# Moving the row sums of four modulation vectors from the DeltaNet heads to the branch merge of a hybrid encoder layer

## The chip, the cores and the metric

The kernel runs on one core of a Trainium2 chip. The metric is the device time of one execution in microseconds (us), as a median over runs. TensorE (PE in the profile) multiplies matrices, VectorE (DVE), ScalarE (ACT) and GpSimd (POOL) work elementwise, and SyncE (SP) issues the DMAs. PE reads from the on-chip memory SBUF and writes to eight PSUM banks of 128 x 512 floats.

## The reference, cut to what matters

One layer with 1024 tokens and a width of 1024. A conditioning vector `c` gives six modulation vectors of 1024 each:

```
mod = silu(c) @ w_ada + b_ada
shift_t, scale_t, gate_t, shift_f, scale_f, gate_f = split(mod, 6)
h = x * (1 + scale_t) + shift_t
proj = h @ w_in            # DeltaNet q,k,v,z; attention q,k,v; merge gates ...
merged = gate_a * (o_a @ w_branch_a) + gate_b * (o_b @ w_branch_b)
x = layernorm(ALPHA * x + gate_t * (merged @ w_o))
h = x * (1 + scale_f) + shift_f
x = layernorm(ALPHA * x + gate_f * ffn(h))
```

`o_a` comes from eight heads of a gated delta rule, `o_b` from sixteen heads of band attention. The first two vectors are needed at once. The last four, `gate_t`, `shift_f`, `scale_f` and `gate_f`, are 4096 columns of `w_ada` (16.8 MB) that are not needed before the output projection `w_o`. The change is about these four.

## The kernel before, in words

The kernel passes through these stages: the first two modulation vectors and `h`; the eight DeltaNet heads; attention in eight pairs of heads; the merge, sixteen branch blocks (eight of `w_branch_a`, then eight of `w_branch_b`); the output projection `mix` with the first layer norm; the up-projection; the down-projection.

Matrices are multiplied as three products of a high and a low part. A weight block of 128 x 1024 floats is loaded into a place called `raw`, ACT casts it to the high part `wh` (L177), and POOL or DVE subtracts to get the low part `wl` or the like (L180). The pool `W` has nine places of 512 KB, W0 to W8: three for `raw` (W0 to W2), three for `wh` (W3 to W5), three for `wl` (W6 to W8). Each call of `W.tile(..., tag="raw", bufs=RB)` takes the next of its three in turn. `place("W0", ...)` names a place directly, and `ring(key, ...)` takes the next place of the list that the table `AT` has under the key. `pbank(name, ring)` does the same with PSUM banks, by the table `RINGS`; there `"po"`, `"i"` and `"mod"` are all bank 7.

The order of the instructions on each engine is made by a planner ahead of the run: it goes through the program with priorities (earlier lines first, some stages raised) and a model of costs, and it puts in every wait. SP issues all DMAs of these stages in one list.

In the heads, `mod_rows(i)` (L803 to L826) is called twice for each head, i from 0 to 15. The 4096 columns are eight strips of 512, and each strip takes two halves of four row blocks of 128. A half loads two raws of 512 KB (L811) from the three-place ring and makes four VectorE passes over 128 x 512 (L816 for the first, L818 for the others), each adding `silu(c)` times a row block to an accumulator in the ring `gt`, which has two places and is shared with the evictions of the merge gates. After an odd half, a matmul with a matrix of ones sums over the 128 partitions (L822, tile `pmod`, bank 7), the bias row is loaded (L824), added (L825) and the strip is stored to `mod_d` in DRAM (L826). Bank 7 is in the heads that of `stage_inverse` too.

In the merge (from L1036), block j of branch br takes its weights by `wblock` (L1041), and two groups of 24 matmuls (L1047) make 512 columns each. The gates come from DRAM (L1051); DVE multiplies (L1053, L1055) and in branch B POOL adds both branches (L1056). At blocks 5, 6 and 7 the eight operands `ob_d` of branch B are loaded and split (L1064); in branch B the eight blocks of `w_o` are loaded (L1073), scaled by `gate_t` (L1074, from `mod_d`) and split. PE works on branch A while attention is still running, since the planner fills with it what attention leaves.

After `mix(0)` and `mix(1)`, `shift_f` and `scale_f` are loaded from `mod_d` as sixteen rows of 128 (L1116), transposed on PE (L1118) and combined with the layer norm's vectors in `aff`.

Of the kernel before, what the change touches and what calls it, by code (L numbers as in the profile page):

```python
# [73 lines left out]
def _at(group, step_, n, first=0):  # L74
# [27 lines left out]
    "bt": _at("GA", 640, 2), "sb": (*_at("GA", 640, 4, 1280), ("FA", 384)),  # L102
    "ot": (("GA", 3840), ("FA", 0)), "mx": _at("FA", 4, 8, 256),

    "gb": _at("GB", 512, 2), "macc": _at("M", 0, 1), 
    "st": _at("ST", 12, 2), "mv": _at("ST", 4, 4, 36), "gtb": (MA[0],), "g1b": (_E1[1],),
    "b1b": (_E1[2],), "r": (_E1[3], ("GL", 0)), "x1": _at("GL", 1024, 2, 1024),
    "h2": _at("GL", 0, 1, 3072),
# [45 lines left out]
def hybrid_layer(  # L154
# [646 lines left out]
    macc = [None]  # L801

    def mod_rows(i):  # L803

        cb = i // 2
        if i % 2 == 0:
            macc[0] = ring("gt", [P, 512])
        acc = macc[0]
        for k0 in range(4 * (i % 2), 4 * (i % 2) + 4, 2):
            rv = W.tile([P, 2, 512], F32, tag="raw", bufs=RB, name=nm("raw"))  # L810
            SP.dma_start(rv, w_ada2[k0 * P:(k0 + 2) * P,  # L811
                                    2 * D + 512 * cb:2 * D + 512 * cb + 512].rearrange(
                                        "(k p) n -> p k n", p=P))
            for k in (k0, k0 + 1):
                if k == 0:
                    DVE.tensor_scalar(acc, rv[:, 0, :], csil[:, 0:1], None, ALU.mult)  # L816
                else:
                    DVE.scalar_tensor_tensor(acc, rv[:, k - k0, :], csil[:, k:k + 1], acc,  # L818
                                             ALU.mult, ALU.add)
        if i % 2 == 1:  # L820
            pr_ = mtile(nm("pmod"), "i")
            PE.matmul(pr_, ones, acc, start=True, stop=True)  # L822
            row = ring("gt", [P, 512])[0:1, :]
            SP.dma_start(row, b_ada[:, 2 * D + 512 * cb:2 * D + 512 * cb + 512])  # L824
            DVE.tensor_tensor(row, row, pr_[0:1, :], ALU.add)  # L825
            SP.dma_start(mod_d[:, 512 * cb:512 * cb + 512], row)  # L826
# [13 lines left out]
    for h in range(HA):  # L840
        ORD = "sigKq"
        for o in ORD:
            if o == "s":
                with tc.high_priority(offset=PF):
                    stage_solve(h, cs[h])
            elif o == "i":
                with tc.high_priority(offset=PI):
                    stage_inverse(h, cs[h])
            elif o == "K" and h + 1 < HA:
                with tc.issue_after(last.ins) if last else nullcontext():  # L850
                    cs.append(stage_k(h + 1))
            elif o == "g":
                some_gates(GA[h])
            elif o == "q" and h + 1 < HA:
                stage_q(h + 1, cs[h + 1])
        some_gates(GB[h])
        for i in (2 * h, 2 * h + 1):
            mod_rows(i)
        if h + 1 < HA:
            stage_vz(h + 1, cs[h + 1])  # L860
        with tc.high_priority(offset=PC):
            stage_chain(h, cs[h])
        with tc.high_priority(offset=PT):
            stage_out(h, cs[h])
        last = cs[h]["last"]
# [150 lines left out]

    oah, oal = hh, hl
    group("GO", "G", 4096, F32R)
    group("M", _E1[4], 1024)
    group("GB", "FT", 1024)  # L1020
    group("ST", "ST", 52)
    ma = [place(o, [P, S], F32, "ma") for o in MA]
# [6 lines left out]
    def bcast(key, src):  # L1029
        t_ = ring(key, [P, D])  # L1030
        SP.dma_start(t_, src.partition_broadcast(P).rearrange("p o n -> p (o n)"))
        return t_

    wo = []
    for br in range(2):
        if br == 1:  # L1036
            mh, ml = (t_.rearrange("p k s -> p (k s)").rearrange("p (t k q) -> p t k q", t=NT, k=NK)
                      for t_ in (hh, hl))
        rh, rl = ((oahk, oalk), (obh, obl))[br]
        for j in range(NK):  # L1040
            w = wblock(kview(wbr[br], j * P, P), NK)  # L1041
            for n in range(2):
                N = slice(512 * n, 512 * n + 512)
                ps = pbank(nm("pbr"), "ab"[br])
                for k in range(NK):
                    for a, r in ((w[0], rh), (w[0], rl), (w[1], rh)):
                        PE.matmul(ps, a[:, k, :], r[k][:, N],  # L1047
                                  start=(k == 0 and a is w[0] and r is rh),
                                  stop=(k == NK - 1 and a is w[1]))
                gt_ = ma[j][:, N] if br == 0 else ring("gb", [P, 512])  # L1050
                SP.dma_start(gt_, gates_d[br * NK + j][:, N])  # L1051
                if br == 0:
                    DVE.scalar_tensor_tensor(gt_, gt_, 1.0, ps, ALU.add, ALU.mult)  # L1053
                else:
                    DVE.scalar_tensor_tensor(gt_, gt_, 1.0, ps, ALU.add, ALU.mult)  # L1055
                    POOL.tensor_tensor(gt_, gt_, ma[j][:, N], ALU.add)  # L1056
                    T4 = slice(4 * n, 4 * n + 4)
                    split(mh[:, T4, j, :], ml[:, T4, j, :],
                          gt_.rearrange("p (t q) -> p t q", t=4), ACT, DVE)
                    if "merged" in dbg:  # L1060
                        SP.dma_start(dbg["merged"][j * P:j * P + P, N], gt_)
            if br == 0:
                for k in {5: (0, 1), 6: (2, 3, 4), 7: (5, 6, 7)}.get(j, ()):
                    load_split(obh[k], obl[k], ob_d[k], ACT, DVE)  # L1064
            if br == 1 and j == 0:
                gtb = bcast("gtb", mod_d[:, 0:D])
                DVE.tensor_scalar(gtb, gtb, 0.5, None, ALU.mult)
            if br == 1 and j and (j % 2 == 0 or j == NK - 1):

                for k in ([j // 2 - 1] if j < NK - 1 else range(3, NK)):  # L1070
                    a, b = (place(o, [P, D], F32R, "wo") for o in (*MA[1:], *OB[:9])[2 * k:2 * k + 2])
                    raw = W.tile([P, D], F32, tag="raw", bufs=RB, name=nm("raw"))
                    SP.dma_start(raw, w_o2[k * P:k * P + P, :])  # L1073
                    DVE.tensor_tensor(raw, raw, gtb, ALU.mult)  # L1074
                    split(a, b, raw, ACT, DVE)
                    wo.append((a, b))
# [542 lines left out]
```

## Time and profile before

| | us |
|---|---|
| median of 3 runs | 2221.7 (2218.23 to 2227.03) |
| profiled execution, its own time | 2219.0 |
| its span | 2217.3 |
| stretch of the heads | 100 to 900 |
| attention without the merge | 900 to 1233 |
| merge beside attention | 1233 to 1340 |
| merge alone | 1340 to 1454 |

A row of a group has the line, the engine, the operation, its shapes and count, then the busy time in us and the mean of one in ns, then the idle time of the engine just before and what ended it. A row of the timeline has its start and its length in us; "x2" means that two were put together, and brackets hold the idle time before it with its releaser. In a table by stretches each engine has its busy time and the count of its instructions, and at the end stand the clock granted to TensorE as a share of full speed, the share of DMA time and GB/s. "PEld" is TensorE's weight load, and a name with q is an engine's own issue queue.

### The profile page before, as it was taken

To read this page: it belongs to the slowest core of one execution; us is meant where nothing else is said; L and a number is where in the kernel's file an instruction comes from. 1 tells how busy PE (TensorE), PEld (TensorE's weight loads), DVE (VectorE), ACT (ScalarE), POOL (GpSimd) and SP (SyncE) were. 2 spreads that over 40 slices of the span, in tenths; PEclk is the share of its full clock that TensorE was granted. 3 is DMA by queue.
4 is the path that set the end of the run, shared out by engine and by line. 5 is a ranking of instruction groups with operands and counts; after the bars stand their busy time and mean duration, and the time that the engine had idled before them with its cause. 6 is when DMAs were issued, how large, how long until landed. Compare 5 with 4: busy or idle time off the path is not lost.

```text
span 2217.3 us, 31612 instructions
## 1 busy us (share of the span) xinstructions
PE 2121.5 (96%) x11469; PEld 1777.6 (80%) x11469; DVE 1559.2 (70%) x3228; ACT 1044.8 (47%) x2216; POOL 580.8 (26%) x544
## 2 busy tenths in 40 slices
PE   6998999999999999999999999999899999999997
PEld 5687787777878787798989788888688888888876
DVE  8567585765667664567676653556998888879897
ACT  4645253434434334467675642234554444446453
POOL 4323232332322232233343522424010000000023
PEclk9999999999999999999999999999999999999999
DMA  9232333423233412211111424342232222254222
GB/s 287 80 110 79 93 93 106 121 75 107 86 92 93 143 36 85 78 56 51 60 57 64 154 90 139 105 142 86 67 105 86 85 72 82 86 203 149 95 95 86
DMA packets 227263, 220.48 MB, mean 99 GB/s; under 512 B 27354, under 2 KB 184467, under 8 KB 227107
## 3 DMA queue, kind: packets, MB, share of 16 engines
q1 hardware_dynamic: 227027, 218.44, 31.1%
q8 instruction: 90, 1.47, 0.3%
q14 instruction: 66, 0.54, 0.1%
q10 hardware_dynamic: 80, 0.03, 0.0%
HBM read 177.48 MB, written 47.23 MB: 101 GB/s over the span
## 4 chain that ended last, share of the span: by engine, by line
PE 43%; DVE 6%; issue 1%; ACT 1%; POOL 1%; DMA 0%; DVEq 0%; ACTq 0%; POOLq 0%
PE pup L1295 18%; PE pbr L1047 8%; PE pwo L1109 4%; PE pdn L1474 4%; PE pqk L884 2%; PE pv L899 2%; PE po L974 2%; PE pp L959 1%; PE ps L933 1%; DVE hl L180 1%; DVE hh L1562 1%; DVE hh L1488 0%; ACT hh L1557 0%; POOL hh L1532 0%; DMA raw<-in_w_branch_a_dram 0%
## 5 line engine op out<-in xcount | busy, mean ns | idle before, releaser
L180 POOL TENSOR_TENSOR wl<-raw,wh 128x1024 fp32r<-128x1024 f32 x88 | 211.8, 2409 | 327.0 <-ACT wh L177 304.6
L1295 PE MATMUL pup<-hh,wop 128*128 128x512 f32 x704 | 226.8, 393 | 0.4 <-ACT hh L177 0.4
L1295 PE MATMUL pup<-t,wop 128*128 128x512 f32 x792 | 191.3, 395 | 5.5 <-DVE wop L180 3.3
L1295 PEld LDWEIGHTS pup<-t,wop 128*128 128x128 f32 x792 | 149.8, 189 | 39.4 <-DVE wop L180 3.7
L1295 PEld LDWEIGHTS pup<-hh,wop 128*128 128x128 f32 x704 | 133.1, 189 | 29.4 <-ACT hh L177 0.8
L177 ACT CAST wh<-raw 128x1024 fp32r<-128x1024 f32 x88 | 92.4, 1050 | 136.2 <-DMA raw<-in_w_in_dram 56.2
L284 PE MATMUL pqkv<-hh,wh 128*128 128x512 f32 x352 | 143.0, 407 | 0.0
L284 PE MATMUL pqkv<-hl,wh 128*128 128x512 f32 x352 | 140.9, 400 | 0.0
L284 PE MATMUL pqkv<-hh,wl 128*128 128x512 f32 x352 | 139.8, 398 | 0.0
L1295 PE MATMUL pup<-hl,wop 128*128 128x512 f32 x352 | 138.1, 392 | 1.7 <-DVE hl L180 1.7
L663 DVE TENSOR_TENSOR FT<-FT,G 128x16 f32<-128x16 f32 (+30 forms) x248 | 121.3, 489 | 17.5 <-POOL G L608 10.2
L177 ACT CAST wop<-wr 128x512 fp32r<-128x512 f32 x110 | 67.8, 622 | 124.7 <-DVE wr L1281 62.8
L944 POOL TENSOR_SCALAR G<-G,FT 128x640 f32<-128x640 f32 (+4 forms) x103 | 70.0, 682 | 182.9 <-DVE FT L943 161.7
L180 DVE TENSOR_TENSOR wop<-wr,wop 128x512 fp32r<-128x512 f32 x110 | 80.9, 741 | 23.8 <-ACT wop L177 23.8
L1336 POOL TENSOR_TENSOR cc<-cc,G 128x512 f32<-128x512 f32 x15 | 26.2, 1748 | 266.7 <-DVE G L1318 223.8
L284 PE MATMUL pgt<-hh,wl 128*128 128x512 f32 x240 | 95.2, 397 | 0.8 <-POOL wl L180 0.8
L284 PE MATMUL pgt<-hh,wh 128*128 128x512 f32 x240 | 95.5, 398 | 0.2 <-DVE tmp L530 0.2
L284 PE MATMUL pgt<-hl,wh 128*128 128x512 f32 x240 | 94.8, 395 | 0.0
L1474 PE MATMUL pdn<-hl 128*128 128x512 f32 x360 | 85.2, 390 | 1.8 <-ACT pdn L1469 1.5
L963 DVE TENSOR_TENSOR pl<-pp,ph 128x512 fp32r<-128x512 f32 (+2 forms) x116 | 72.5, 635 | 17.4 <-ACT ph L962 16.6
L1474 PEld LDWEIGHTS pdn<-hl 128*128 128x128 f32 x360 | 67.4, 188 | 16.6 <-ACT pdn L1469 1.9
L941 ACT ACTIVATE G<-G,FT 128x640 f32<-128x640 f32 (+4 forms) x103 | 71.6, 696 | 18.9 <-DVE FT L936 16.9
(465 smaller groups left out, 6139.8 us busy)
## 6 DMA issues: line engine op xcount, KB each, us to landing
raw<-in_w_in_dram SPq DMA_DIRECT2D x72, 512.0 KB
wr<-in_w_up_dram SPq DMA_DIRECT2D x44, 512.0 KB
raw<-in_w_ada_dram SPq DMA_DIRECT2D x32, 512.0 KB
dr<-g_d SPq DMA_DIRECT2D x18, 512.0 KB
dr<-in_w_down_dram SPq DMA_DIRECT2D x18, 512.0 KB
wa<-in_w_ada_dram SPq DMA_DIRECT2D x32, 256.0 KB
gates_d<-GT SPq DMA_DIRECT2D x32, 256.0 KB
g_d<-yy SPq DMA_DIRECT2D x15, 512.0 KB
```

The costliest lines, as they stand in the source:

```text
L177: ACT.copy(h, src)
L180: return le.tensor_tensor(l, src, f(h), ALU.subtract).ins
L284: PE.matmul(ps, a[:, k, :], r[k][:, 512 * n:512 * n + 512], start=(k == 0 and a is wh and r is rh), stop=(k == NK - 1 and a is wl))
L663: DVE.tensor_tensor(pr[:, :, 0:i + 1], ft[:, :, 0:i + 1], fa[:, i:i + 1, 0:i + 1].to_broadcast([P, 8, i + 1]), ALU.mult)
L884: PE.matmul(ps, a[:, k, :], r[:, k, 512 * n:512 * n + 512], start=(k == 0 and a is w[0] and r is hh), stop=(k == NK - 1 and a is w[1]))
L941: ACT.activation(sb[:, 0:n], sb[:, 0:n], AF.Exp, bias=mx[:, nb - 1:nb], scale=-1.0, accum_out=mx[:, 2:3])
L944: POOL.tensor_scalar(sb[:, 0:n], sb[:, 0:n], mx[:, 3:4], 0.0, ALU.mult, ALU.add)
L963: DVE.tensor_tensor(pl[:, B, :], pp, f(ph[:, B, :]), ALU.subtract)
L1047: PE.matmul(ps, a[:, k, :], r[k][:, N], start=(k == 0 and a is w[0] and r is rh), stop=(k == NK - 1 and a is w[1]))
L1109: PE.matmul(ps[n], a[:, t, k, :], wo[k][b][:, 512 * n:512 * n + 512], start=(k == 0 and a is mh and b == 0), stop=(k == NK - 1 and a is ml))
L1295: PE.matmul(ps, a[:, u, k, :], b[v][k], start=(new and k == 0 and u == 0 and v == 0), stop=(k == 3 and u == 1), skip_group_check=not new)
L1474: PE.matmul(sets[s_][i], a[:, u, i * P:i * P + P], b[:, v, :], start=(new and not seed and j == 0 and u == 0 and v == 0), stop=(j == len(q ...
```

## The change

`mod_rows` and its calls in the heads are taken out. The merge calls `mod_half(i)` after branch blocks 1 to 13, by the table `HALVES`. The accumulators have a ring of two places in W8. Branch blocks get their weights by `branch_block`, with two places each for raw, high and low part (W0 and W1, W3 and W4, W6 and W7) where there were three; the loads of `ob_d` and `w_o` take turns on W0 and W1 with them. Strips 2 to 5 (`shift_f`, `scale_f`) are summed by sixteen products of 128 columns of the accumulator with one column of ones, which leave the result in columns, and the bias is added from the table `vt`; they are not stored to `mod_d`, and its reload with the transpose goes. The other strips are summed and stored as before, with the bias row loaded into the accumulator's first row.

The diff holds the new functions twice, in the same function body and ahead of the loop that calls them. `mod_half` stands first with raws from the ring `mraw` (W2 and W5) and without the sum, which `mod_sum` then makes a block later; it stands again with raws from the three-place ring and with the sum at the end of the odd half, and `macc` is set again, to a list with one element, where it was a dictionary. In the loop, `mod_sum` is called for a strip number that is found in `macc`.

```
-    "gb": _at("GB", 512, 2), "macc": _at("M", 0, 1), 
+    "gb": _at("GB", 512, 2), "macc": _at("MA", 512, 2), "mraw": ("W2", "W5"), "mw0": ("W0", "W1"),
+    "mwh": ("W3", "W4"), "mwl": ("W6", "W7"),
...
-        for i in (2 * h, 2 * h + 1):
-            mod_rows(i)
...
+    group("MA", "W8", 1024)
+    macc = {}
+
+    def mod_half(i):
+
+        cb = i // 2
+        if i % 2 == 0:
+            macc[cb] = ring("macc", [P, 512])
+        acc = macc[cb]
+        for k0 in range(4 * (i % 2), 4 * (i % 2) + 4, 2):
+            rv = ring("mraw", [P, 2, 512])
...
+    def mod_sum(cb):
...
+    HALVES = {1: [0], 2: [1], 3: [2], 4: [3], 5: [4], 6: [5], 7: [6], 8: [7, 8], 9: [9], 10: [10, 11], 11: [12],
+              12: [13, 14], 13: [15]}
+    nmod = [0]
+
+    def sp_raw(h, l, src, he, le):
+        raw = ring("mw0", [P, 1024])
+        SP.dma_start(raw, src)
+        split(h, l, raw, he, le)
+
+    def branch_block(i):
+        raw = ring("mw0", [P, NK, P])
+        SP.dma_start(raw, kview(wbr[i // NK], i % NK * P, P))
+        wh, wl = (ring(o, [P, NK, P], F32R) for o in ("mwh", "mwl"))
+        split(wh, wl, raw, ACT, POOL)
+        return wh, wl
...
+    macc = [None]
+
+    def mod_half(i):
+
+
+        cb = i // 2
+        if i % 2 == 0:
+            macc[0] = ring("macc", [P, 512])
+        acc = macc[0]
+        for k0 in range(4 * (i % 2), 4 * (i % 2) + 4, 2):
+            rv = W.tile([P, 2, 512], F32, tag="raw", bufs=RB, name=nm("raw"))
...
+        if i % 2 == 0:
+            return
+        pr_ = pbank(nm("pmod"), "mod")
+        if 2 <= cb < 6:
+            for q in range(4):
+                PE.matmul(pr_[:, q:q + 1], acc[:, q * P:q * P + P], ones[:, 0:1], start=True, stop=True)
+            o, v = 8 + 4 * (cb - 2), VO["b_ada"] + 16 + 4 * cb
+            DVE.tensor_tensor(aff[:, o:o + 4], pr_[:, 0:4], vt[:, v:v + 4], ALU.add)
+        else:
+            PE.matmul(pr_, ones, acc, start=True, stop=True)
+            row = acc[0:1, :]
+            SP.dma_start(row, b_ada[:, 2 * D + 512 * cb:2 * D + 512 * cb + 512])
+            DVE.tensor_tensor(row, row, pr_[0:1, :], ALU.add)
+            SP.dma_start(mod_d[:, 512 * cb:512 * cb + 512], row)
...
-            w = wblock(kview(wbr[br], j * P, P), NK)
+            w = branch_block(NK * br + j)
...
+            for cb in range(nmod[0]):
+                if cb in macc and macc[cb] is not None:
+                    mod_sum(cb)
+                    macc[cb] = None
+            for i in HALVES.get(NK * br + j, ()):
+                mod_half(i)
+                nmod[0] = (i + 1) // 2
             if br == 0:
                 for k in {5: (0, 1), 6: (2, 3, 4), 7: (5, 6, 7)}.get(j, ()):
-                    load_split(obh[k], obl[k], ob_d[k], ACT, DVE)
+                    sp_raw(obh[k], obl[k], ob_d[k], ACT, DVE)
...
-                    raw = W.tile([P, D], F32, tag="raw", bufs=RB, name=nm("raw"))
+                    raw = ring("mw0", [P, D])
...
-    mrow = ring("macc", [P, P])[0:16, :]
-    SP.dma_start(mrow, mod_d[:, D:3 * D].rearrange("o (r p) -> (o r) p", p=P))
-    pmr = pbank("pmr", "t")
-    PE.transpose(pmr[:, 0:16], mrow, ident[0:16, 0:16])
...
+    DVE.tensor_scalar(s1, s1, 1.0, None, ALU.add)
+    DVE.tensor_tensor(g1f, s1, b1c, ALU.mult)
+    DVE.tensor_tensor(b1f, b1f, g1f, ALU.add)
     DVE.tensor_tensor(g1f, s1, g1c, ALU.mult)
```

More of the change, by code (lines that the diff above doesn't have):

```diff
@@ L799, in gate_block @@
             SP.dma_start(gates_d[j][:, N], gt_)
[L801 to L826, printed above, removed]
     gate_block(0)
@@ L1018, in hybrid_layer @@
     group("GO", "G", 4096, F32R)
-    group("M", _E1[4], 1024)
     group("GB", "FT", 1024)
@@ L1032, in bcast @@
         return t_
+    aff = cst.tile([P, 24], F32, tag="aff", name="aff")
+    group("MA", "W8", 1024)
[7 more added lines that the diff above has]
+            rv = ring("mraw", [P, 2, 512])
+            SP.dma_start(rv, w_ada2[k0 * P:(k0 + 2) * P,
+                                    2 * D + 512 * cb:2 * D + 512 * cb + 512].rearrange(
+                                        "(k p) n -> p k n", p=P))
+            for k in (k0, k0 + 1):
+                if k == 0:
+                    DVE.tensor_scalar(acc, rv[:, 0, :], csil[:, 0:1], None, ALU.mult)
+                else:
+                    DVE.scalar_tensor_tensor(acc, rv[:, k - k0, :], csil[:, k:k + 1], acc,
+                                             ALU.mult, ALU.add)
@@ new lines, in mod_sum @@
+    def mod_sum(cb):
+        acc = macc[cb]
+        pr_ = pbank(nm("pmod"), "mod")
[4 more added lines that the diff above has]
+            DVE.tensor_tensor(aff[:, o:o + 4], pr_[:, 0:4], vt[:, v:v + 4], ALU.add)
+        else:
+            PE.matmul(pr_, ones, acc, start=True, stop=True)
[3 more added lines that the diff above has]
+            SP.dma_start(mod_d[:, 512 * cb:512 * cb + 512], row)
@@ new lines, in bcast @@
+    def bcast(key, src):
+        t_ = ring(key, [P, D])
+        SP.dma_start(t_, src.partition_broadcast(P).rearrange("p o n -> p (o n)"))
+        return t_
+    aff = cst.tile([P, 24], F32, tag="aff", name="aff")
+    macc = [None]
[6 more added lines that the diff above has]
+            rv = W.tile([P, 2, 512], F32, tag="raw", bufs=RB, name=nm("raw"))
+            SP.dma_start(rv, w_ada2[k0 * P:(k0 + 2) * P,
+                                    2 * D + 512 * cb:2 * D + 512 * cb + 512].rearrange(
+                                        "(k p) n -> p k n", p=P))
+            for k in (k0, k0 + 1):
+                if k == 0:
+                    DVE.tensor_scalar(acc, rv[:, 0, :], csil[:, 0:1], None, ALU.mult)
+                else:
+                    DVE.scalar_tensor_tensor(acc, rv[:, k - k0, :], csil[:, k:k + 1], acc,
+                                             ALU.mult, ALU.add)
+        if i % 2 == 0:
+            return
+        pr_ = pbank(nm("pmod"), "mod")
+        if 2 <= cb < 6:
+            for q in range(4):
+                PE.matmul(pr_[:, q:q + 1], acc[:, q * P:q * P + P], ones[:, 0:1], start=True, stop=True)
+            o, v = 8 + 4 * (cb - 2), VO["b_ada"] + 16 + 4 * cb
+            DVE.tensor_tensor(aff[:, o:o + 4], pr_[:, 0:4], vt[:, v:v + 4], ALU.add)
+        else:
+            PE.matmul(pr_, ones, acc, start=True, stop=True)
+            row = acc[0:1, :]
+            SP.dma_start(row, b_ada[:, 2 * D + 512 * cb:2 * D + 512 * cb + 512])
+            DVE.tensor_tensor(row, row, pr_[0:1, :], ALU.add)
+            SP.dma_start(mod_d[:, 512 * cb:512 * cb + 512], row)
@@ L1114, in hybrid_layer @@
     ps, nxt = mix(0), mix(1)
-    mrow = ring("macc", [P, P])[0:16, :]
-    SP.dma_start(mrow, mod_d[:, D:3 * D].rearrange("o (r p) -> (o r) p", p=P))
-    pmr = pbank("pmr", "t")
-    PE.transpose(pmr[:, 0:16], mrow, ident[0:16, 0:16])
-    aff = cst.tile([P, 24], F32, tag="aff", name="aff")
-    g1f, b1f, s1 = aff[:, 0:8], aff[:, 8:16], aff[:, 16:24]
+    b1f, s1, g1f = aff[:, 8:16], aff[:, 16:24], aff[:, 0:8]
     g1c, b1c = vt[:, VO["ln1g"]:VO["ln1g"] + 8], vt[:, VO["ln1b"]:VO["ln1b"] + 8]
-    DVE.tensor_scalar(s1, pmr[:, 8:16], 1.0, None, ALU.add)
+    DVE.tensor_scalar(s1, s1, 1.0, None, ALU.add)
+    DVE.tensor_tensor(g1f, s1, b1c, ALU.mult)
+    DVE.tensor_tensor(b1f, b1f, g1f, ALU.add)
     DVE.tensor_tensor(g1f, s1, g1c, ALU.mult)
-    DVE.tensor_tensor(b1f, s1, b1c, ALU.mult)
-    DVE.tensor_tensor(b1f, pmr[:, 0:8], b1f, ALU.add)
     late, t2f = [], []
```

## The prediction

> **What bounds the kernel now.** I read the page's engine shares first.
>
> ```profile
> span 2217.3 us, 31612 instructions
> PE 2121.5 (96%) x11469; PEld 1777.6 (80%) x11469; DVE 1559.2 (70%) x3228; ACT 1044.8 (47%) x2216; POOL 580.8 (26%) x544
> ```
>
> TensorE (PE) sets the time, so an edit counts by the PE work that it takes away and by the PE holes that it closes or opens. Next, the busy time by stretches: heads (100 to 900), attention, the part of attention in which the merge already runs, and the rest of the merge.
>
> ```profile
> core 0: us, PE busy (x) PEld busy (x) DVE busy (x) ACT busy (x) POOL busy (x), PEclk, DMA share, GB/s
> 100.00:900.00 800.00, 768.23 (x4631) 639.04 (x4630) 523.23 (x1322) 325.14 (x896) 233.77 (x234) 0.99 0.32 94
> 1233.00:1340.00 107.00, 102.79 (x557) 87.69 (x556) 59.79 (x154) 54.70 (x108) 41.50 (x34) 0.95 0.40 131
> 1340.00:1454.00 114.00, 114.00 (x506) 94.13 (x505) 50.57 (x52) 27.13 (x33) 39.19 (x23) 1.00 0.39 124
> ```
>
> The heads, which lose work, hold 31.8 us of PE holes (800 - 768.23). The merge after 1340, which gets work, has none: its loads are hidden. The same stretches for the merge's matmuls alone:
>
> ```profile
> 1233.00:1340.00 107.00, 67.41 (x270) 50.11 (x270) 7.55 (x11) 0.95 0.40 131
> 1340.00:1454.00 114.00, 113.53 (x498) 93.46 (x498) 13.69 (x20) 1.00 0.39 124
> ```
>
> A block is 48 matmuls, 48 x 113.53/498 = 10.9 us. By 1340 the PE has done 270/48 = 5.6 blocks, so without new holes block 7 begins at 1355.4 and block 8 at 1366.3.
>
> **The heads.** What leaves, by groups in 100 to 900, and what the PE waited for there:
>
> ```profile
> L818 DVE SCALAR_TENSOR_TENSOR GT<-raw,csil,GT 128x512 f32<-128x512 f32 x56 | 43.4, 776 | 3.5 <-DMA raw<-in_w_ada_dram 2.2
> L822 PE MATMUL pmod<-GT,ones 128*128 128x512 f32 x16 | 8.2, 592 | 0.0
> L825 DVE TENSOR_TENSOR GT<-GT,pmod 1x512 f32<-1x512 f32 x8 | 5.4, 672 | 3.7 <-PE pmod L822 3.7
> L816 DVE TENSOR_SCALAR GT<-raw,csil 128x512 f32<-128x512 f32 x8 | 3.9, 484 | 19.8 <-DMA gates_d<-GT 15.8 <-DMA qk_d<-GT 4.0
> PE pxt L687 <- DMA G<-ft_d: 9.3, 9, 2.7
> PE pvn L729 <- DVE vs L726: 6.5, 8, 2.6
> ```
>
> 8.2 us of PE leave. 52.7 us of VectorE (43.4 + 5.4 + 3.9) and its 19.8 us of waiting for a gate's store leave too; of the PE holes only the last two rows hang on them, 15.8 us at most. I take 4, because the row sits at the solve's own DMA trip more than at VectorE. Heads: -12.2, bounds -24.0 and 0 (the planner makes a new order for all that is left, and that may eat it).
>
> **The places.** By the diff the change is not what its words say. `mod_half` is defined twice in one function, and the calls come after both, so the second counts: it takes its raws from the old three-place ring (W0, W1, W2), not from W2 and W5, and it sums at once; `mod_sum` is never reached. Branch blocks and the `ob_d` and `w_o` loads take turns on W0 and W1 of the same three. The ring has given 3 + 47 + 28 + 8 = 86 places (first blocks, heads, attention, branch-A operands) before; 86 mod 3 = 2, so halves take (W2,W0), (W1,W2), (W0,W1) and so on. The planner gives a place in the order of the program, and each load waits for the one before it there:
>
> ```profile
> 1302.46 2.39 POOL L180 TENSOR_TENSOR wl<-raw,wh 128x1024 fp32r<-128x1024 f32 x1 [0.26 <-ACT wh L177]
> 1304.87 11.24 SPq L185 DMA_DIRECT2D raw<-in_w_branch_a_dram  x2
> ```
>
> The load at 1304.87 goes out when the subtract on its place ends (1304.85). The same for PSUM bank 7, which head 7's inverse and its `pmod` share:
>
> ```profile
> 767.76 0.74 DVE L818 SCALAR_TENSOR_TENSOR GT<-raw,csil,GT 128x512 f32<-128x512 f32 x1
> 850.50 0.68 PE L713 MATMUL pT<-G 128*64 128x64 f32 x8
> 856.26 1.02 PE L822 MATMUL pmod<-GT,ones 128*128 128x512 f32 x2
> ```
>
> The accumulator was ready at 768.5, and the sum ran only after the inverse's last tile. In the changed kernel the sums are in bank 7 behind every attention output `po`, whose last reader is:
>
> ```profile
> 1341.27 0.36 ACT L979 COPY FT<-po 64x256 f32<-64x256 f32 x1
> 1342.53 0.43 DVE L980 TENSOR_TENSOR ob<-po,FT 64x256 f32<-64x256 f32 x1
> ```
>
> So no sum runs before 1343.0. Two accumulators hold strips 0 and 1; half 4, called in block 5, needs the first back. Its two raws land early and sit on W1 and W2 until then, and behind them queue, on W1, the loads of ob1, ob2, ob4, ob5, ob7 and branch block 9. Half 5 puts raws on W0 and W1, with ob3, block 7, ob6 and block 8 behind.
>
> **One turn of a place.** Issue to use of 512 KB:
>
> ```profile
> 1342.53 0.33 SPq L185 DMA_DIRECT2D raw<-ob_d  x1
> 1348.24 1.63 SPq L185 DMA_DIRECT2D raw<-ob_d  x2
> 1452.64 0.38 SPq L1251 DMA_DIRECT2D wr<-in_w_up_dram  x1
> 1346.95 1.05 ACT L177 CAST ob<-raw 128x1024 fp32r<-128x1024 f32 x1 [5.33 <-DMA raw<-ob_d]
> 1351.50 1.06 ACT L177 CAST G<-raw 128x1024 fp32r<-128x1024 f32 x1 [3.50 <-DMA raw<-ob_d]
> 1457.55 0.62 ACT L177 CAST wop<-wr 128x512 fp32r<-128x512 f32 x1 [4.47 <-DMA wr<-in_w_up_dram]
> 1348.30 1.23 DVE L180 TENSOR_TENSOR ob<-raw,ob 128x1024 fp32r<-128x1024 f32 x1 [3.11 <-DMA ob_d<-ob]
> L1074 DVE TENSOR_TENSOR raw<-raw,gtb 128x1024 f32<-128x1024 f32 x8 | 9.8, 1226 | 10.9 <-DMA raw<-in_w_o_dram 10.9
> L180 DVE TENSOR_TENSOR wo<-raw,wo 128x1024 fp32r<-128x1024 f32 x8 | 14.1, 1769 | 6.1 <-POOL FT L1056 4.4 <-ACT wo L177 1.7
> ```
>
> 4.4, 3.3 and 4.9 us. I take 3.8, the mean of the two `ob_d` loads, bounds 3.3 and 4.9. A turn is then 6.1 for an ob (cast 1.05, subtract 1.23), 5.3 for a modulation raw (two passes of 0.75), 7.25 for a branch block (1.05, 2.4), 7.85 for a `w_o` block (1.23, 1.05, 1.77). The Trainium skill (DMA: Bandwidth & Descriptors, "Anatomy of one DMA") fits 2.0 us plus bytes at 436 GB/s for a DMA of another path, 3.2 us here by my estimate; the rows lie above it. By it, nine loads in a row on W1 would give 5.4 us less stall.
>
> **Small transfers and the clock.**
>
> ```profile
> L608 POOL MEMSET G<- 128x32 f32 x8 | 1.3, 162 | 21.3 <-DMA G<-fa_d 17.0 <-PE pvn L729 4.3
> 1248.00:1253.00 5.00, 2.94 (x16) 2.53 (x15) 2.36 (x7) 2.65 (x7) 1.25 (x1) 0.84 1.05 340
> 1253.00:1258.00 5.00, 5.00 (x20) 4.09 (x20) 3.98 (x11) 4.88 (x10) 4.86 (x7) 0.70 0.76 232
> L397 PE MATMUL pmods<-ones,G x32: 165/250/374, 10.5 to 58.0; 128*128 128x1 f32 x32
> ```
>
> A small round trip costs at least 17.0/8 = 2.1 us, which I take. After a PE hole of 2.06 us the granted clock was 0.70 over 5 us, a loss of 1.5 us.
>
> **The chain after attention.** First sum 1343.0 to 1344.0, bias row in 1346.1, add 1346.8, row out 1349.4 with its issue. Half 4 frees W1 at 1350.6 and W2 at 1352.1. W1: ob1 1356.7, raw of half 5 1362.0, ob2 1368.1, ob4 1374.2, ob5 1380.3, ob7 1386.4. W0: half 5 1353.6, ob3 1359.7, block 7 ready 1367.0, half 6 1372.3, ob6 1378.4, block 8 ready 1385.6. So block 7 begins 11.5 us late, and after it (1377.9) block 8 finds a second hole of 7.7. Block 9 follows two halves on W1 and is ready at 1404.2, when block 8 has ended at 1396.5: 7.7 more. From then on each place is ready just in time (blocks 13 and 14 to the microsecond, with the `w_o` turns). Together 26.9 us. Bounds: 22 with loads of 3.3; with 4.9, ten more, and 3 each at blocks 13 and 14, 43. If half 4 doesn't wait, 0.
>
> SP's queue is one list, too: gate loads sit behind a waiting raw, and evictions (L1053, L1055) behind those; the PE is by then already waiting for weights, so this costs nothing of its own.
>
> The clock after three holes: 3 x 1.5 = 4.5 us, bounds 0 and 6. The Trainium skill (TensorE: Matmul & The Clock Gate, "What's actually happening") has half speed after an idle window, and about 3.4 us to return, an estimate of 1.7 us a time, 5.1; the row agrees.
>
> **The sums, and what stays hidden.** Four row sums are half of L822's 8.2, 4.1 us. The other four become 16 one-column products, 32 records of the kind that L397 has, at its median of 0.25 us 8.0. Of these 12.1 about half falls into the holes (strips 0 to 3 are summed there): +6, bounds 0 and 12.1. VectorE's 52.7 us go where it is busy 59.79 of 107 and 50.57 of 114, 74% with it; the matmuls of that stretch cover it, and if attention's steps had to wait for it, the 16 passes of halves 0 to 3, 0.75 each, would cost 12 us. The 16.8 MB of loads add about 93 GB/s over 180 us to some 130; the 1248 row shows 340 GB/s. Two `wh` places instead of three still let block j+1 be cast while block j runs (3.5 us under 10.9). The `mod_d` reload with its transpose goes; it was behind `mix(0)`: 0.
>
> Sum in the profiled execution's own time, 2219.0: -12.2 + 26.9 + 4.5 + 6 = +25.2, 2244.2. The median of before lies 2.7 above that execution: 2247.
>
> **Rivals.**
> - *The other side:* the heads decide. If freed VectorE time closes all 15.8 us of holes, the gain is 24.0; it wins once stalls, clock and sums stay below 13 us. For it: 2.7 us is the longest wait, small delays that a free VectorE ends. Against it: half 4's place in bank 7. Time 2221.7 - 24.0 + 6 of sums + 4 of stall = 2208. Chance 0.15.
> - *Partly hidden:* the planner brings more branch blocks before half 4's raws or attention ends earlier against the merge, so that only one hole of about 11.5 stays: 2221.7 - 12.2 + 11.5 + 6 = 2227. Against it: the places' order is the program's. Chance 0.15.
> - *As its words say:* raws on W2 and W5 and sums a block later. Then half 4 still waits, but nothing queues behind: 2221.7 - 12.2 + 6 = 2216. The second definition speaks against it. Chance 0.03.
> - *Worse:* turns of 4.9 us in all the merge, stalls of 43: 2247 + 16 = 2263, or more with DMA contention in blocks with two halves. Chance 0.12.
>
> **Numbers.** The forecast has 0.55, its own range 2228 to 2264. From 2208 (the first rival) to 2270 (the worse one with some contention) no more than 2 in 10 is left out. A median 0.5% off (11 us) is about what a measurement can tell from no change. Faster: the first rival, 0.15. Within 0.5%: the second and third, 0.18. Slower: the forecast and the last, 0.67.
>
> **What would show it.** Right: `pmod` beginning only after the last `po`; raw loads of ob and branch blocks 7 to 9 waiting on the subtracts and modulation passes of the place before; PE waiting for `wh` in the branch matmuls by 20 to 30 us in all after attention, in two or three holes of 8 to 12 with a clock below 1. Heads: PE idle of 24 to 30 us. Wrong: a full PE through the merge, `pmod` between `po` matmuls, raws on W5, or heads that change by more than 24 us.

## The result, and the profile after

The changed kernel takes 2251.15 us (median of four, 2248.83 to 2252.75) beside 2220.99 for the kernel before (2218.23 to 2227.03): a ratio of 1.0135, 95% interval 1.0120 to 1.0149, 30.2 us slower. The forecast was 2247, slower.

The page of the changed kernel, its span and its engines:

```profile
span 2247.8 us, 31664 instructions
PE 2135.1 (95%) x11492; PEld 1782.5 (79%) x11492; DVE 1553.5 (69%) x3228; ACT 1042.8 (46%) x2218; POOL 581.4 (26%) x544
```

The same work is done in 30.5 us more span. TensorE is busy 13.6 us longer, though there is little more for it to do, and the rest is idle. The table by stretches of the changed kernel, for the stretches that the prediction used, says where:

```profile
100.00:900.00 800.00, 773.77 (x4728) 645.69 (x4726) 483.03 (x1282) 339.02 (x936) 234.58 (x238) 1.00 0.26 75
1233.00:1340.00 107.00, 106.30 (x557) 90.07 (x556) 59.42 (x139) 37.45 (x75) 29.18 (x25) 0.97 0.47 149
1340.00:1454.00 114.00, 95.03 (x375) 75.46 (x375) 65.06 (x82) 18.89 (x23) 31.20 (x18) 0.88 0.55 178
```

The holes (time in which TensorE is idle) shrink in the heads from 31.8 to 26.2 us, and in the merge beside attention from 4.2 to 0.7 us. The stretch of the merge alone, which was full, has 19 us of holes and a granted clock of 0.88. TensorE's rows in the timeline of the changed kernel (the last attention output, the first sum, the first matmuls of blocks 8 and 9, the last of block 15):

```profile
1311.60 0.27 PE L946 MATMUL po<-ph,v 128*128 128x128 f32 x1
...
1316.98 1.02 PE L1096 MATMUL pmod<-W,ones 128*128 128x512 f32 x2
...
1356.76 2.08 PE L1115 MATMUL pbr<-ob,mwh 128*128 128x512 f32 x4 [4.92 <-ACT mwh L178]
...
1377.43 2.08 PE L1115 MATMUL pbr<-ob,mwh 128*128 128x512 f32 x4 [5.74 <-ACT mwh L178]
...
1480.14 0.39 PE L1115 MATMUL pbr<-G,mwl 128*128 128x512 f32 x1
```

and of the kernel before, for the first, third and last of these:

```profile
1340.05 0.27 PE L974 MATMUL po<-ph,v 128*128 128x128 f32 x1
...
1366.07 0.63 PE L1047 MATMUL pbr<-ob,wh 128*128 128x512 f32 x2
...
1453.31 0.39 PE L1047 MATMUL pbr<-G,wl 128*128 128x512 f32 x1
```

Branch A ends at 1351.8 (1356.76 less the hole of 4.92), 14.2 us ahead of before. Branch B then takes 128.7 us (to 1480.53) in place of 87.6. So 14.2 are won up to there, 41.1 are lost in branch B, and the remaining 3.6 behind it. The busy time of the branch matmuls in that stretch (first two rows) and of `mix` (third row), and then of the branch matmuls before:

```profile
1357.00:1400.00 43.00, 34.29 (x124) 26.48 (x125) 0.82 0.63 200
1400.00:1480.60 80.60, 64.72 (x262) 50.60 (x260) 0.94 0.45 148
...
1400.00:1480.60 80.60, 7.87 (x26) 5.52 (x26) 0.94 0.45 148
```

```profile
1366.00:1454.00 88.00, 87.69 (x386) 71.96 (x384) 1.00 0.34 110
```

The same eight blocks keep TensorE busy for 99.3 us (0.3 of it before 1357) where it was 87.7, at a clock of 0.82 and 0.94 where it was 1.00. These 11.6 us I put down to the clock; by its two shares alone, 34.29 x 0.18 + 64.72 x 0.06, it would be 10.1. 7.9 us are matmuls of `mix` that the planner has pulled in among the blocks, so they are not lost here; but `mix` and what follows lose 3.6 us although they have 7.9 us less to do. The holes come from the table by stretches:

```profile
1357.00:1380.00 23.00, 16.90 (x64) 13.36 (x65) 12.82 (x18) 3.33 (x4) 6.61 (x4) 0.80 0.59 190
1380.00:1400.00 20.00, 19.68 (x77) 16.10 (x78) 11.69 (x16) 2.62 (x3) 6.43 (x4) 0.85 0.68 211
1400.00:1420.00 20.00, 16.84 (x79) 13.72 (x77) 13.14 (x19) 3.52 (x5) 6.82 (x5) 1.00 0.57 183
1420.00:1440.00 20.00, 17.35 (x66) 13.52 (x67) 10.10 (x12) 3.74 (x6) 5.63 (x5) 0.91 0.42 138
1440.00:1460.00 20.00, 18.19 (x65) 13.69 (x65) 10.80 (x12) 2.48 (x4) 7.92 (x5) 0.83 0.43 139
...
1480.00:1500.00 20.00, 15.85 (x61) 12.05 (x60) 13.88 (x15) 5.43 (x7) 1.59 (x1) 0.91 0.58 202
```

From 1357 to 1460 they come to 14.0 us; with the 4.9 before block 8 that is 18.9. The 41.1 are thus 18.9 of holes, 11.6 of clock, 7.9 of `mix`, and 2.7 left for the sums. At the start of `mix`, 1480 to 1500, stand 4.2 more. What TensorE waited for, in the list of waits from 1225 to 1520:

```profile
PE pbr L1115 <- ACT mwh L178: 17.2, 5, 5.7
...
PE pwo L1184 <- ACT wo L178: 3.2, 2, 2.4
```

Five waits for a cast of branch weights, of at most 5.7 us. SP's rows in the timeline show what makes these casts late:

```profile
1352.24 0.38 SPq L1056 DMA_DIRECT2D mw<-in_w_branch_b_dram  x1
...
1359.18 9.17 SPq L1078 DMA_DIRECT2D raw<-in_w_ada_dram  x5
1372.88 0.37 SPq L1056 DMA_DIRECT2D mw<-in_w_branch_b_dram  x1
```

Block 9's load goes out at 1372.88, behind five modulation raws, and 4.6 us later TensorE starts the block. VectorE's rows show what it waited for:

```profile
1370.84 0.75 DVE L1085 SCALAR_TENSOR_TENSOR W<-raw,csil,W 128x512 f32<-128x512 f32 x1 [2.88 <-DMA raw<-in_w_ada_dram]
1371.51 0.68 DVE L1123 SCALAR_TENSOR_TENSOR FT<-FT,pbr 128x512 f32<-128x512 f32 x1
1372.10 0.74 DVE L1085 SCALAR_TENSOR_TENSOR W<-raw,csil,W 128x512 f32<-128x512 f32 x1
```

The load goes out as the modulation pass of the third row ends (1372.84).

### The profile page after: what moved, and what is told of

It reads as the page before. It is cut to its first block, busy times and chain, and to the rows that moved or that the text cites. A ratio compares the mean times of both kernels' runs of the same rounds, so it can differ in the third digit from the quotient of the medians.

```text
span 2247.8 us, 31664 instructions
## 1 busy us (share of the span) xinstructions
PE 2135.1 (95%) x11492; PEld 1782.5 (79%) x11492; DVE 1553.5 (69%) x3228; ACT 1042.8 (46%) x2218; POOL 581.4 (26%) x544
## 5 line engine op out<-in xcount | busy, mean ns | idle before, releaser
L181 POOL TENSOR_TENSOR wl<-raw,wh 128x1024 fp32r<-128x1024 f32 x72 | 172.8, 2402 | 255.1 <-ACT wh L178 240.5
L664 DVE TENSOR_TENSOR FT<-FT,G 128x16 f32<-128x16 f32 (+30 forms) x248 | 121.7, 491 | 12.2 <-POOL G L609 5.0
L178 ACT CAST wh<-raw 128x1024 fp32r<-128x1024 f32 x72 | 75.6, 1050 | 90.4 <-PE pgt L285 37.8
L1406 POOL TENSOR_TENSOR cc<-cc,G 128x512 f32<-128x512 f32 x15 | 26.2, 1750 | 267.8 <-DVE G L1388 224.6
L935 DVE TENSOR_TENSOR pl<-pp,ph 128x512 fp32r<-128x512 f32 (+2 forms) x116 | 72.5, 635 | 18.9 <-ACT ph L934 18.4
L1184 PE MATMUL pwo<-wo,hh 128*128 128x512 f32 x256 | 77.5, 407 | 5.0 <-ACT wo L178 3.2
L1115 PE MATMUL pbr<-ob,mwh 128*128 128x512 f32 x192 | 66.1, 434 | 16.5 <-ACT mwh L178 16.5
```

Source lines behind the costliest of these rows:

```text
L178: ACT.copy(h, src)
L181: return le.tensor_tensor(l, src, f(h), ALU.subtract).ins
L664: DVE.tensor_tensor(pr[:, :, 0:i + 1], ft[:, :, 0:i + 1], fa[:, i:i + 1, 0:i + 1].to_broadcast([P, 8, i + 1]), ALU.mult)
L935: DVE.tensor_tensor(pl[:, B, :], pp, f(ph[:, B, :]), ALU.subtract)
L1115: PE.matmul(ps, a[:, k, :], r[k][:, N], start=(k == 0 and a is w[0] and r is rh), stop=(k == NK - 1 and a is w[1]))
L1184: PE.matmul(ps[n], a[:, t, k, :], wo[k][b][:, 512 * n:512 * n + 512], start=(k == 0 and a is mh and b == 0), stop=(k == NK - 1 and a is ml))
```

## The experiments

Each run stands beside runs of the kernel before on the same chip; the chips differ between runs. The last column is the difference of the two medians; the text below adds and subtracts it. The intervals reach 2 to 5 us to either side, so what is subtracted between two runs is good to some 4 to 6 us.

| run | median, us | ratio and 95% interval | against before, us |
|---|---|---|---|
| the change | 2251.2 | 1.0135 (1.0120 to 1.0149) | +30.2 |
| 1 raws of their own | 2245.1 | 1.0114 (1.0094 to 1.0133) | +26.5 |
| 2 the change as worded | 2244.7 | 1.0109 (1.0089 to 1.0129) | +26.2 |
| 3 before, two places each | 2244.6 | 1.0113 (1.0094 to 1.0132) | +26.0 |
| 4 before, no vectors in the heads | 2203.6 | 0.9928 (0.9905 to 0.9951) | -15.0 |
| 5 three shared places | 2253.9 | 1.0149 (1.0132 to 1.0166) | +33.4 |
| 6 before, two raw places | 2244.8 | 1.0102 (1.0087 to 1.0118) | +24.3 |
| 7 before, two places of the halves | 2222.1 | 1.0008 (0.9997 to 1.0018) | +1.6 |
| 8 the change without loads and passes | 2224.1 | 1.0011 (1.0002 to 1.0021) | +3.6 |
| 9 three raws, and own ones | 2233.7 | 1.0058 (1.0043 to 1.0073) | +12.0 |
| 10 as 9, ScalarE's queue | 2234.0 | 1.0063 (1.0044 to 1.0083) | +12.3 |
| 11 as 9, halves spread evenly | 2231.7 | 1.0046 (1.0030 to 1.0063) | +10.0 |
| 12 as 9, narrow passes | 2223.4 | 1.0006 (0.9994 to 1.0018) | +2.8 |

**1. Raws of their own.** The modulation's raws leave the ring of the branch blocks:

```
-            rv = W.tile([P, 2, 512], F32, tag="raw", bufs=RB, name=nm("raw"))
+            rv = ring("mraw", [P, 2, 512])
```

> The changed kernel with the modulation's raws on W2 and W5 and nothing else on these two; sums still at the end of the odd half. Theory A (raws share W0 and W1 with branch blocks and operands, so a branch block's load stands behind them): the holes of branch B go, what is left is the gain before the merge (some 15 to 17 us) less the sums (some 6): 2210 us, 2203 to 2217. Theory B (the 16.8 MB themselves, on the DMA engines or in SP's one list, slow every other load of the merge, whatever place they land in): 2235 to 2250.

2245.1. The prediction's mechanism, loads that queue on W0 and W1 behind half 4's raws, is gone here, and only 3.7 of the 30.2 us go with it, with intervals that overlap. Branch B's first and last matmul in the timeline of this run:

```profile
1358.90 0.63 PE L1115 MATMUL pbr<-ob,mwh 128*128 128x512 f32 x2
...
1472.31 0.39 PE L1115 MATMUL pbr<-G,mwl 128*128 128x512 f32 x1
```

It still takes 113.8 us. The holes before blocks 8 and 9 are gone; the longest wait for a cast now stands at a later block:

```profile
1419.14 2.07 PE L1115 MATMUL pbr<-ob,mwh 128*128 128x512 f32 x4 [8.50 <-ACT mwh L178]
```

**2. The change as worded.** The second definitions are taken out, so the first ones count: raws on W2 and W5, sums a block later.

```
-    macc = [None]
-    def mod_half(i):
...
-            SP.dma_start(mod_d[:, 512 * cb:512 * cb + 512], row)
```

> The changed kernel with the second definition of the half removed, so that it does what its words say: raws on W2 and W5, and each strip's sum a block later. Theory A: as e1_own or up to 3 us below it, 2207 us. A rival, that the sum's place in the program matters (a sum at the end of its own half stands in TensorE's list ahead of the next block's matmuls and waits for VectorE): 5 us or more below e1_own. Theory B: 2235 to 2250.

2244.7, the same as run 1. Where the sums stand doesn't matter here to within the intervals.

**3. The kernel before, with two places each.** No modulation is moved; the merge only loses its third places:

```
+    "mw0": ("W0", "W1"), "mwh": ("W3", "W4"), "mwl": ("W6", "W7"),
...
-            w = wblock(kview(wbr[br], j * P, P), NK)
+            w = branch_block(NK * br + j)
```

> The kernel before, with the row sums left in the heads, but with the merge's two places each for raw, high and low part instead of three, and the operands and w_o blocks in turns on the same two. Theory A: a third place is not needed when no modulation raw stands between, at most 5 us above the kernel before (2219 to 2226). Rival: the lost third place alone makes the holes of branch B: 2235 to 2250.

26.0 us slower: the part of the change that the prediction put at nothing costs nearly as much as the whole change.

**4. No vectors in the heads.** The loads, passes and sums over partitions of `mod_rows` are left out of the kernel before, and nothing takes their place.

> The kernel before without the row sums of the four vectors (their loads, VectorE passes and partition sums are left out; the strips hold the bias alone). It gives what the heads and attention gain by the removal. The prediction's step: 12 us, 2209. What the two traces suggest: 17 us, 2204. Only the matmuls' time: 8 us, 2213. All holes of the heads: 24 us, 2197.

15.0 us faster. The heads in the table by stretches, and TensorE's timeline of this run:

```profile
100.00:900.00 800.00, 775.38 (x4703) 646.63 (x4701) 479.81 (x1269) 335.20 (x925) 234.08 (x237) 0.99 0.25 75
```

```profile
1350.50 0.63 PE L1030 MATMUL pbr<-ob,wh 128*128 128x512 f32 x2
...
1437.74 0.39 PE L1030 MATMUL pbr<-G,wl 128*128 128x512 f32 x1
```

Block 8 starts 15.6 us earlier than before, and branch B takes 87.6 us. All of the gain is made ahead of the merge, and none is lost there. By this run, that is what moving the vectors could bring if they cost nothing where they go.

**5. Three shared places.** The change with `wblock` and `load_split` as before (three places each), which the modulation's raws share, and with the accumulators in their old slot:

```
-    group("MA", "W8", 1024)
+    group("MA", _E1[4], 1024)
...
     def branch_block(i):
-        raw = ring("mw0", [P, NK, P])
...
+        return wblock(kview(wbr[i // NK], i % NK * P, P), NK)
```

> The changed kernel, but with the merge on the three raw places and the three places of each half that it had before, shared by branch blocks, branch B's operands, w_o's rows and the modulation's raws; the accumulators move from the third place of the low halves to the slot that held them before. Nothing of the modulation moves back. Theory 'places' (the third places that the change takes from the branch blocks are what costs; the run of the kernel before with two places each cost 26 us, the run without the modulation in the heads gained 15): about 2208 to 2222, not slower than before, with branch B's blocks within 95 us instead of 129. Rival 'the modulation itself in the merge' (its 16 loads of 512 KB and 32 passes on VectorE cost the same wherever they lie, since they hold the queue of the loads): 2235 to 2250, and branch B's blocks still above 105 us.

2253.9 (three executions; a fourth took 11477.5 us and is left out), no faster than the change itself, where 2208 to 2222 was expected from the places alone. (The texts of runs 5 and 8 to 10 count 16 loads, the first two also 32 passes; there are 32 and 64.) In its waits of TensorE a new one leads:

```profile
PE pmod L1090 <- DVE B L1079: 22.7, 4, 8.7
```

`pmod` is the tile of the sums: the planner put sums ahead of branch matmuls in TensorE's list, and they waited for passes that waited for their loads. So the run doesn't separate the two theories: it gives three places back, but it makes the sums late.

**6 and 7. Which lost place costs.** Run 3 taken apart: in run 6 only the raws have two places, in run 7 only the halves of the weights.

```
 run 6   raw = ring("mw0", ...)                       wh, wl on three places as before
 run 7   raw = W.tile(..., tag="raw", bufs=RB)        wh, wl = ring("mwh", ...), ring("mwl", ...)
```

> The kernel before, with the raws of the merge's blocks, branch B's operands and w_o's rows on two places, and the weights' halves on three as before. With two places of both it was 26 us slower. Theory 'raws': the third raw is what lets a load start while one raw is being cast and one waits, so nearly all of the 26 us comes back here: 2238 to 2246. Rival 'halves': the halves are held through the 10.9 us of a block's matmuls, so the third of them is what counts, and here the time stays within 6 us of the kernel before: 2218 to 2225.

> The kernel before, with the weights' halves of the merge's blocks on two places each, and all raws on three as before. Theory 'halves': nearly all of the 26 us, 2236 to 2246. Rival 'raws': 2218 to 2225. If both runs lie between, the two lost places share the cost: their sum above the kernel before should then come to about 26 us.

24.3 us and 1.6 us, 25.9 together, as in run 3. It is the third raw. Where run 6 loses it, in its table by stretches:

```profile
1440.00:1460.00 20.00, 18.26 (x81) 14.68 (x80) 7.60 (x7) 4.61 (x6) 7.78 (x4) 1.00 0.28 88
1460.00:1480.00 20.00, 12.91 (x55) 9.78 (x53) 11.18 (x13) 3.66 (x6) 5.44 (x4) 0.90 0.43 145
1480.00:1500.00 20.00, 15.88 (x52) 11.79 (x52) 11.09 (x16) 5.42 (x7) 0.00 (x0) 0.75 0.44 149
```

13.0 us of holes at the step from the merge into `mix`, with a clock down to 0.75 (before, TensorE has none from 1440 to 1500). The loads of `w_o` in this run, and then in the kernel before (count, durations of the issue, first and last start; of eight loads these traces have seven):

```profile
L1086 SPq DMA_DIRECT2D mw<-in_w_o_dram x7: 328/333/377, 1390.7 to 1491.9; - x7
```

```profile
L1073 SPq DMA_DIRECT2D raw<-in_w_o_dram x7: 328/333/428, 1404.6 to 1461.9; - x7
```

The last five of the eight stand behind block 15 in the program. A row's place is held for 7.85 us by the prediction's own turn, so five rows need by this estimate 13 us on three places and 20 on two. The last load goes out 8.2 us after the last branch matmul before (1461.9 - 1453.7) and 21.5 us after it in run 6, whose last one ended at 1470.4. The other part stands at the start: block 8 begins at 1374.2, 8.1 us later than before. But most of that is no wait for a place. Up to 1220, before any branch matmul, in the kernel before and then in run 6:

```profile
0.00:1220.00 1220.00, 1152.83 (x7093) 979.19 (x7094) 809.06 (x2107) 582.51 (x1482) 387.53 (x414) 0.99 0.31 93
```

```profile
0.00:1220.00 1220.00, 1153.00 (x7062) 978.40 (x7063) 804.53 (x2095) 578.80 (x1474) 386.76 (x411) 0.98 0.31 93
```

In the same busy time 31 matmuls fewer are done, about 5 us by the mean of 0.163 us. The edit touches nothing there but the planner's order (the clock is 0.98 in place of 0.99), so of the 24.3 us some 19 are left for the third raw in the merge and behind it.

**8. The change without its loads and passes in the merge.** The accumulators are set to zero once; places, sums and bias stay.

```
-        for k0 in range(4 * (i % 2), 4 * (i % 2) + 4, 2):
...
+        if i % 2 == 0:
+            DVE.memset(acc, 0.0)
```

> The changed kernel, with the 16 loads of the modulation's weights and the 32 passes over them left out of the merge (an accumulator is set to zero once; the sums over partitions, the bias and the places stay as changed), so that the four vectors hold the bias alone. Theory 'two costs' (two places 26 us; the loads and passes beside the branch blocks another 15 to 20; the heads give 15 back): 2225 to 2232, with no half-speed windows of TensorE in branch B but the tail into the output projection as in the run with two places. Rival 'places alone' (the loads and passes cost nothing, and the rest is the order in which the queues now run): 2243 to 2251.

+3.6. Against run 4 the places (with the sums) cost 18.6 us here, and the loads and passes are the other 26.6 of the change. Of run 6's two losses only the second is left, and 18.6 us, sums included, is near the 19 above. The wait of `mix` in TensorE's timeline, and the loads of `w_o`:

```profile
1459.70 2.08 PE L1174 MATMUL pwo<-wo,hh 128*128 128x512 f32 x4 [6.76 <-ACT wo L178]
```

```profile
L1138 SPq DMA_DIRECT2D mw<-in_w_o_dram x6: 328/333/373, 1407.5 to 1469.6; - x6
```

**9 to 11. Better places, another queue, another spread.** Run 9 is the change as worded, with three raws for the branch blocks, two places of each half, and the modulation's raws on the two places that this leaves. Run 10 issues their loads from ScalarE's queue, run 11 puts one half beside each block from the first on.

```
 run 9   "mraw": ("W5", "W8"), raw = W.tile(..., tag="raw", bufs=RB), group("MA", _E1[4], 1024)
 run 10  -            SP.dma_start(rv, w_ada2[...
         +            ACT.dma_start(rv, w_ada2[...
 run 11  HALVES = {**{j: [j] for j in range(14)}, 14: [14, 15]}
```

> The changed kernel with other places: the branch blocks, branch B's operands and w_o's rows have the three raw places of before; the halves of the weights have two each; the modulation's raws have two of their own (the third places of the halves), the accumulators the slot they had before, and each sum over partitions comes a block after its passes. Theory 'raw places' (a third raw place was worth 24 us, a third place of the halves 1.6; the modulation costs only by what it takes from the raws): 2203.5 without the modulation, 1.6 for the halves and up to 8 for its loads, so 2203 to 2213, faster than before. Rival 'one queue' (its 16 loads stand in the one queue with the gates' and the branch blocks' loads, and each of them that waits for its place holds what is behind it, whatever places there are): 2218 to 2238, with TensorE still waiting for casts in branch B.

> The run above, with the modulation's 16 loads issued from ScalarE's queue in place of SyncE's; nothing else. Theory 'one queue': at least 10 us below the run above, toward 2205 to 2215, as the gates and the branch blocks no longer stand behind a raw that waits for its place. Rival 'raw places': within 3 us of the run above. A third way: the waits for a place now hold ScalarE's casts instead, and it is as slow as or slower than the run above, by up to 15 us.

> The first of these runs with the modulation's halves spread one to a block from the first block on (blocks 0 to 13, two beside block 14), in place of one a block from the second on with two beside blocks 8, 10 and 12. Theory 'one queue, and what is doubled up in branch B decides': 5 to 15 us below the first run. Rival 'the amount decides, not its place': within 3 us of the first run.

With the raws given back, 18.2 us of the change's loss go, but run 9 is still 12.0 us slower than before. By runs 4 and 7 it would be at -13.4 if the modulation cost nothing in the merge, so it costs 25.4 there with its sums, about the 26.6 that it costs in the change without them. (The text of run 12 has 28, from medians of two chips.) The queue isn't why (run 10, +0.3), nor is the doubling up beside blocks 8, 10 and 12 (run 11, 2.0 less, with intervals that overlap). None of these beats the kernel before.

**12. Narrow passes.** Run 9 with each pass over 8 columns in place of 512; the loads and waits stay, and the rest of the pass is left out.

```
-                    DVE.scalar_tensor_tensor(acc, rv[:, k - k0, :], csil[:, k:k + 1], acc, ...
+                    DVE.scalar_tensor_tensor(acc[:, 0:8], rv[:, k - k0, 0:8], csil[:, k:k + 1], acc[:, 0:8], ...
```

> The kernel with three raw places, two places of each half and own raws for the modulation (2233.7), with its 64 passes narrowed from 512 columns to 8: the 32 loads of 512 KB, the waits for them, the number of instructions and the sums over partitions stay, and an accumulator is set to zero first; left out is the rest of each pass, so the four vectors are not the reference's. That kernel stands 28 us above what the parts without the modulation in the merge give (2203.5 without it in the heads, and 1.6 for the halves' places). Theory 'VectorE': the passes, 1.0 us each there, stand in VectorE's one list ahead of the evictions, subtracts and scalings that TensorE waits for; without their time nearly all of the 28 us goes: 2203 to 2212. Rival 'loads': the 16.8 MB, the waits of VectorE for them and SyncE's list cost it: 2224 to 2234. Between these the two share it.

2223.4, +2.8: between the two ranges, 0.6 us below that of 'loads'. The groups of passes in run 9, then in run 12, from 1300 to 1500:

```profile
L1024 DVE SCALAR_TENSOR_TENSOR B<-mraw,csil,B 128x512 f32<-128x512 f32 x56 | 55.2, 986 | 19.0 <-DMA mraw<-in_w_ada_dram 18.1
```

```profile
L1025 DVE SCALAR_TENSOR_TENSOR B<-mraw,csil,B 128x8 f32<-128x8 f32 x56 | 23.5, 420 | 27.6 <-DMA mraw<-in_w_ada_dram 26.4 <-DVE B L1025 0.2
```

Taking 31.7 us of passes from VectorE gives 9.2 us back. 16.2 us stay with the loads, VectorE's waits for them (now 26.4 us), what is left of the passes, and the sums. Which of these it is, is open.

## Why the prediction was right, and where its steps were not

**The heads: right, slightly too small.** -12.2 was predicted; run 4 measured -15.0, with an interval that reaches 5 us to either side. The changed kernel's idle time of 26.2 us in the heads lies in the 24 to 30 that the prediction named. That the gain survives the planner's new order was right too.

**The places: the step that failed.** "Two `wh` places instead of three still let block j+1 be cast while block j runs" is right (run 7, 1.6 us). But the prediction priced only these. It worked out a turn of the raw places (5.3 to 7.85 us) and then asked only who stands behind whom on two of them, starting from half 4, and put the tail with `w_o` "just in time". The loss of the third raw place costs 24.3 us (run 6) without any modulation, some 5 of them ahead of the merge; all lost places and the sums together cost 18.6 in the change (run 8 less run 4).

**The stalls: size near, cause wrong.** 26.9 us of stalls were predicted, 11.5 at block 7, 7.7 each at blocks 8 and 9, since half 4 was to wait for bank 7 until 1343. The first sum did run only behind the last `po`, as predicted, but attention ended 28 us earlier and the sum ran at 1317; block 7 started with no such hole. That is the condition of the rival "partly hidden", yet not its result. The holes came in branch B and in `mix`, 18.9 + 4.2 us, none over 5.8. Before blocks 8 and 9, where 7.7 us each were predicted, stand 4.9 and 5.7, and block 9's load did wait for a modulation pass on its place: there the predicted queue is real. It was priced too high, because a block was called ready only after its subtract (7.25 us after the load); TensorE starts 4.5 us after it (1352.24 to 1356.76), when the cast is done. Nor does the time hang on this queue alone: run 1, which undoes the sharing on which the step rested, gives 3.7 back, and another wait of 8.5 us takes the place of these two. In place of the predicted stalls the runs put two costs: the lost third raw place, and the modulation's loads and passes beside the blocks.

**VectorE and the loads: wrong.** The prediction let TensorE's matmuls cover VectorE's 52.7 us and 16.8 MB of loads, cost 0. They cost 26.6 in the change (run 8) and 25.4 on better places (run 9), of which 9.2 are the passes' width. Why an engine that is busy for 65.06 of 114 us holds the path is in the group of passes of the changed kernel, from 1320 to 1490:

```profile
L1085 DVE SCALAR_TENSOR_TENSOR W<-raw,csil,W 128x512 f32<-128x512 f32 x42 | 32.3, 771 | 17.2 <-DMA raw<-in_w_ada_dram 16.5
```

VectorE stood 16.5 us for their loads, and what is behind a pass in its list stands too. The rows from 1370.84 show one such case: the eviction of block 8's first half (L1123) starts at 1371.51, straight behind a pass that had waited 2.88 us, though its last matmul had ended at 1365.4.

**The clock: right in kind, too small.** 4.5 us for three holes at 1.5 were predicted; 11.6 came in branch B alone.

**The sums: within the bounds, but worked out too large.** TensorE's busy time with the one-column sums (L1092), then with the others (L1096):

```profile
1300.00:1500.00 200.00, 4.54 (x32) 5.08 (x32) 0.92 0.52 169
```

```profile
1300.00:1500.00 200.00, 4.08 (x8) 1.50 (x8) 0.92 0.52 169
```

That is 8.6 us where 12.1 was worked out. The others take the 4.1 of the prediction; the 32 one-column records of 0.25 us overlap and take 4.5 together, not 8.0. How much of it lies on the path was not measured by itself.

**The sum.** Measured by runs: -15.0 (run 4) + 18.6 (run 8 less run 4) + 26.6 (the change less run 8) = +30.2; that it closes is by construction, and only the split is measured. Predicted: -12.2 + 26.9 + 4.5 + 6 = +25.2. That the total came out near was luck: 37.4 us of stalls, clock and sums, reached by a chain of which only a part happened, stood against 45.2 us, most of it costs that had been put at nothing. The forecast's sign was no accident, since the changed merge does wait for its raws. The rival on the other side fell: the heads do give 15, but its 10 us of sums and stall were 45.

## What to carry to other kernels

A place that is taken away is priced where its users come thickest: here the holes that the third raw left stood not among the steady blocks, but at the step into the output projection (13 us), where five loads stand together. Work that is moved to an idle engine's time stands in that engine's list with its waits: count what is queued behind it, and not the engine's share of busy time. Before a move, run the kernel without the moved work, and without the room that the move needs: these two runs (-15 and +26) already give the sign, though not the other 19 us, which the moved work costs in its new place.

## What was not expected of the hardware

**A hole costs more than itself.** The changed kernel's table in steps of 2 us around block 9's hole of 5.74 us:

```profile
1374.00:1376.00 2.00, 0.00 (x0) 0.00 (x0) 1.96 (x4) 0.62 (x1) 0.00 (x0) 0.95 0.85 258
1376.00:1378.00 2.00, 0.57 (x1) 0.50 (x2) 1.90 (x4) 1.04 (x1) 0.76 (x1) 0.50 0.70 197
...
1384.00:1386.00 2.00, 2.00 (x6) 1.56 (x5) 0.69 (x1) 0.44 (x1) 1.43 (x1) 0.50 0.76 257
1386.00:1388.00 2.00, 2.00 (x10) 1.60 (x10) 0.24 (x1) 0.00 (x0) 1.48 (x1) 0.99 0.05 19
```

The granted clock is at 0.50 from some 1375.8, within the hole, until 1386 (0.95 and 0.99 in the first and last row). From TensorE's restart at 1377.4 that is 8.6 us, of which it is busy for 8.3, so about 4.1 us are lost beside the hole. The Trainium skill (TensorE: Matmul & The Clock Gate, "What's actually happening") gives about 3.4 us of activity to return; after this hole it took more than twice that, with one more hole of 0.3 us in it. The prediction's 1.5 us came from a hole of 2.06 us.

**A pass of VectorE that meets GpSimd waits for it.** A pass of 0.75 us by itself in run 9 (VectorE, then GpSimd), and one of 0.23 us in run 12:

```profile
1345.71 2.80 DVE L1024 SCALAR_TENSOR_TENSOR B<-mraw,csil,B 128x512 f32<-128x512 f32 x1 [2.16 <-DMA mraw<-in_w_ada_dram]
```

```profile
1345.56 2.39 POOL L181 TENSOR_TENSOR mwl<-raw,mwh 128x1024 fp32r<-128x1024 f32 x1 [13.79 <-ACT mwh L178]
```

```profile
1347.02 2.27 DVE L1025 SCALAR_TENSOR_TENSOR B<-mraw,csil,B 128x8 f32<-128x8 f32 x1 [1.83 <-DMA mraw<-in_w_ada_dram]
```

```profile
1346.88 2.38 POOL L181 TENSOR_TENSOR mwl<-raw,mwh 128x1024 fp32r<-128x1024 f32 x1 [13.42 <-ACT mwh L178]
```

They take 2.80 and 2.27 us: each ends (1348.51 and 1349.29) only when the subtract on GpSimd has ended (1347.95 and 1349.26), within one pass's time after it, and the 8 columns save little. In run 9, ten of the group's 56 passes take 1.2 to 3.0 us, and each of the ten overlaps a subtract or an addition on GpSimd; none of the other 46 is over 0.76. So the group's mean is 0.99 us where it is 0.77 in the changed kernel. The Trainium skill (SBUF — State Buffer, "Who interferes with whom") has a VectorE instruction with two inputs in SBUF contend with a GpSimd instruction that reads SBUF, and the trace agrees. How much of the 25 us of the modulation in the merge comes from this was not tried.
